# First loads in halves over two queues: x's first chunk and the first weights' columns, and the first products in halves, of a hybrid encoder

## The chip, the cores and the metric

The kernel runs on one core of a Trainium2 chip. A core has TensorE (PE, matrix products; the load of its stationary operand is shown as PEld), VectorE (DVE), ScalarE (ACT), GpSimd (POOL) and SyncE (SP), which mostly issues loads. ScalarE can issue loads too, through a queue of its own. The metric is the time of one execution on the device in microseconds (us); lower is better.

## The reference

The reference is a two-layer encoder trunk over 512 tokens of width 1024, in float32. The first layer mixes the tokens by a bidirectional gated linear attention, the second by grouped-query softmax attention with rotary positions. Each is followed by a gated MLP with a width-3 convolution. Before every sub-layer stands an RMS norm. Cut to the part that this change touches, the start of the first layer:

```python
h = rmsnorm(x, norm_mix[0])              # x: (1, 512, 1024)
proj = h @ gla_w_in                      # width 512 + 512 + 1024 + 1024 + 32
q, k, v, g, r = jnp.split(proj, ...)     # v and g: 1024 columns each
...
x = x + gla_mixer(h, ...)
x = x + conv_ffn(rmsnorm(x, norm_ffn[0]), ...)
```

## The kernel before, in words

x is held transposed, features in partitions, as eight chunks of 128 features by 512 tokens (`x[0]` to `x[7]`). Every product is made of three products in a fast 32-bit format (`F32R`): an operand is split into a rounded high part (`hi`, `wh`) and the remainder as low part (`lo`, `wl`), and high by high, high by low and low by high are summed. Of the norm, only the weight per feature is applied ahead of the products; the factor per token comes afterwards.

**The weights.** The class `Weights` loads blocks of 1 MB (`raw`, two buffers) and splits halves of them into `wh` and `wl` (three buffers each). The high part is a copy on ScalarE (line 143, one on VectorE at line 141 for the first), the low part a subtraction on VectorE (line 144).

**The start.** ScalarE's queue issues the load of the parameters `prm` (line 166), among them the norm's weights. SyncE's queue issues eight pairs of loads (lines 170 and 171): chunk c of x, and the 512 columns of the first weights that belong to chunk c. Each load has 256 KB. Each load counts up one of eight counters in turn, and an issue waits until the load before on its counter has landed. Meanwhile PE makes eight small warm-up products from constants (line 182), whose result also gives the constant `halfneg` (line 184, a copy on VectorE).

**The first products.** `gla` (line 343 on) makes the high part of chunk 0 (`norm.high`, line 231, ScalarE), splits the first weights (`W.make`), makes the low part (`norm.low`, line 236, VectorE) and goes on with the other seven chunks. The squares for the norm (line 240 on ScalarE, line 244 summed on VectorE) come beside it. `token_steps` makes the products `vg` (line 297) of the first 512 columns of v: for each chunk k of features, and each of four blocks j of 128 tokens, the block of x is PE's stationary operand and the weights' 512 columns are streamed; four banks collect the sums over all eight chunks. For the first two chunks the products stand by kind: four high by high, then four with `wl`, then four with the low part of x.

**What sets the order.** A scheduler places each engine's instructions by its own estimates of when their operands are ready; the program's order is a guide only. An instruction without inputs, such as the preload of a table of functions for ScalarE (in `gla` and in `attention`), can be placed far ahead. In the order built of the kernel before, the preload of `attention` coincides with the first one (line 411), and one load stands at the start.

Of the kernel before, what the change touches and what calls it, by code (L numbers as in the profile page):

```python
# [8 lines left out]
F32 = mybir.dt.float32  # L9
F32R = mybir.dt.float32r  # L10
U8 = mybir.dt.uint8
AF = mybir.ActivationFunctionType
ALU = mybir.AluOpType

P = 128
S = 512
D = 1024
KC = D // P
NT = S // P
# [27 lines left out]
def hybrid_encoder_kernel(  # L47
# [21 lines left out]
    pe, act, dve, pool, sync = nc.tensor, nc.scalar, nc.vector, nc.gpsimd, nc.sync  # L69
    mm = pe.matmul  # L70
# [7 lines left out]
    def nm(s):  # L78
        uid[0] += 1
        return f"{s}{uid[0]}"  # L80
# [6 lines left out]
    def pair(tag, bufs, dt, n):  # L87
        return sp.tile([P, 2 * S], dt, tag=tag, bufs=bufs, name=nm(n))
# [11 lines left out]
    x = [cp.tile([P, S], F32, name=f"x{c}") for c in range(KC)]  # L100
    prm = cp.tile([P, PC_N], F32, name="prm")

    class Weights:
# [10 lines left out]
        def make(self, key):  # L114
            src, i, h = key
            if h == 0 and (id(src), i) not in self.raw:
                t = sp.tile([P, 4 * S], F32, tag="raw", bufs=2, name=nm("raw"))
                sync.dma_start(t, src[i])
                self.raw[id(src), i] = t
            r = self.raw[id(src), i][:, h * 2 * S : (h + 1) * 2 * S]  # L120
            hi, lo = pair("wh", 3, F32R, "wh"), pair("wl", 3, F32R, "wl")
            if any(src is a and i < n for a, n in self.by_dma):
                act.activation(hi, r, AF.Copy)
                act.activation(lo, r, AF.Copy, scale=-1.0)
                self.pending.append((lo, r))
            else:
                self.split(hi, lo, r, 2 if src is w_vg and i < 2 else 1, src is w_vg and i == 0 and h == 0)
            self.made[id(src), i, h] = (hi, lo)

        def flush(self):  # L130
# [2 lines left out]
                pool.dma_start(lo.bitcast(F32), r, accum_op=ALU.add)  # L133
            self.pending = []

        def split(self, hi, lo, r, pieces, first):
            n = 2 * S // pieces
            for q in range(pieces):
                sl = slice(q * n, (q + 1) * n)
                if first and q == 0:  # L140
                    dve.tensor_copy(hi[:, sl], r[:, sl])
                else:
                    act.activation(hi[:, sl], r[:, sl], AF.Copy)  # L143
                dve.tensor_tensor(lo[:, sl], r[:, sl], hi[:, sl].bitcast(F32), ALU.subtract)  # L144

        def half(self, src, n):
            key = (id(src), n // 2, n % 2)
# [7 lines left out]
    W = Weights()  # L155
# [9 lines left out]

    act.dma_start(prm, par)
    raw = [sp.tile([P, 4 * S], F32, tag="raw", bufs=2, name=f"first{i}") for i in range(2)]
    for c in range(KC):
        r = slice((c % 4) * S, (c % 4 + 1) * S)
        sync.dma_start(x[c], xT[c * P : (c + 1) * P, :])  # L170
        sync.dma_start(raw[c // 4][:, r], w_vg[c // 4, :, r])
        W.raw[id(w_vg), c // 4] = raw[c // 4]

    ident = cp.tile([P, P], F32, name="ident")
    make_identity(nc, ident)
# [34 lines left out]
    class Norm:  # L210
# [15 lines left out]
        def weight(self, c):  # L226
            return prm[:, PC_NORM + self.idx * KC + c : PC_NORM + self.idx * KC + c + 1]

        def high(self, c):
            t = pair("xhl", 8, F32R, "xhl")  # L230
            act.activation(t[:, :S], x[c], AF.Copy, scale=self.weight(c))
            self.hl[c] = (t[:, :S], t[:, S:])

        def low(self, c):
# [48 lines left out]
    def token_steps(src, i0, hl, ps, width, per_half):  # L283

        for hf in range(KC // per_half):
            wh, wl = W.half(src, i0 + hf)

            late = src is w_vg and i0 > 0 and hf == 0
            for kk in range(per_half):
                todo = [(kk, j, i) for j in range(NT - late) for i in range(3)]  # L290
                if late and kk == 1:
                    todo += [(k, NT - 1, i) for k in range(2) for i in range(3)]
                if src is w_vg and i0 + hf * per_half + kk < 2:
                    todo.sort(key=lambda a: a[2])
                for a, j, i in todo:
                    k, sl = hf * per_half + a, slice(a * width, (a + 1) * width)
                    mm(ps[j][:, :width], hl[k][i == 2][:, j * P : (j + 1) * P], (wl if i == 1 else wh)[:, sl],  # L297
                       start=k == 0 and i == 0, stop=k == KC - 1 and i == 2)
                if kk == 1:
                    W.flush()  # L300
                yield

    def token_tiles(*a):
        for _ in token_steps(*a):
            pass
# [35 lines left out]


    def gla(norm, nxt):
        norm.high(0)
        W.make(W.todo.pop(0))
        norm.low(0)
        for c in range(1, KC):
# [7 lines left out]
        def seg(i, between=None):  # L355
            ps = [bank(tag, "vg") for tag in SEG_BANKS[i]]
            for n, _ in enumerate(token_steps(w_vg, i * 4, norm.hl, ps, S, 2)):
                if between is not None:
                    between(n)
            return ps  # L360
# [8 lines left out]
        ps = seg(0)  # L369
# [266 lines left out]
    def attention(norm, nxt):  # L636
# [74 lines left out]
        def kpair():  # L711
            head, ksc = yield from roped(0, PC_QK + 2, 1.0, "ksc")
            ky, kk = [head(0)], []
            yield
            ky.append(head(1))
            for e in range(2):
                yield
                ps = bcast_rows([ksc[:, 2 * j + e : 2 * j + e + 1].to_broadcast([P, P]) for j in range(NT)])
                dve.tensor_tensor(ky[e], ky[e], ps, ALU.mult)
                t = big(F32R, "k")  # L720
                split(ky[e], t)
                kk.append(t)
            return kk
# [3 lines left out]
        def qpair(i, tag="acc"):  # L727
            head, sc = yield from roped(1 + i, PC_QK, float(HD), "qsc", tag)
            for e in range(2):
                y = head(e)  # L730
                yield
                t = big(F32R, "q")
                split(y, t)
                heads[2 * i + e] = (t, sc, e)
                yield
# [17 lines left out]

        ps = [bank("acc" if j < 2 else "pt", "av") for j in range(NT)]
        vg2 = token_steps(w_av, 0, norm.hl, ps, 2 * HD, 4)
        run(qg, 2)
        run(vg2, 1)
# [50 lines left out]
        def mix(h, hf):  # L808
            ph3, pl3 = pts.pop((h, hf))
            vo = (h // 4) * HD  # L810
            if hf == 0:
                pos[h] = bank("po", "po")
            dst = pos[h][:, hf * 256 : (hf + 1) * 256]
            for k in range(NT):
                vsl = slice(k * 256 + vo, k * 256 + vo + HD)
                mm3(dst, vh[:, vsl], vl[:, vsl], ph3[:, k, :], pl3[:, k, :], k == 0, k == NT - 1)
            if hf == 1:
                t = big(F32R, "oT") if h < 4 else pair("xhl", 8, F32R, "oT")
                split(pos[h], t)
                oh[h] = (t[:, :S], t[:, S:])  # L820
# [26 lines left out]

    norms = [Norm(i) for i in range(4)]
    cw = gla(norms[0], norms[1])
    ffn(0, norms[1], cw, norms[2])  # L850
    attention(norms[2], norms[3])
# [82 lines left out]
```

## Time and profile before

| | |
|---|---|
| median of 3 runs | 1133.32 us (1133.29 to 1133.46) |
| the profiled execution | 1133.16 us |
| its span | 1131.4 us |
| PE busy | 1125.7 us |
| DVE busy | 690.1 us |
| ACT busy | 482.1 us |
| POOL busy | 76.0 us |

The span runs from the first instruction to the last of the profiled execution; the time of the execution has some more around it. In a row of the timeline stand start and busy time in us, the engine, the line of the kernel, the operation, its output and its inputs, the shapes, and in brackets the idle time of the engine before it with what ended it. Engines with a q behind their name (SPq, ACTq) are the issue of loads. Several equal instructions that follow each other share a row (x4).

### The profile page before, as it was taken

The page shows a single profiled execution, that of the slowest core. Times are in us where ns is not written, and L with a number is a line of the kernel's source. Part 1 is how long each engine was busy: PE and PEld are TensorE (multiplying, and loading weights), DVE is VectorE, ACT ScalarE, POOL GpSimd, SP SyncE. Part 2 cuts the span into 40 slices and gives each one's busy share as a digit, 9 for nine tenths or more (in the row PEclk, how much of TensorE's full clock was granted, in tenths as well). Part 3 has the DMA queues.
Part 4 walks back from the last instruction along what each step waited for, and adds up shares of the span by engine and source line. Part 5 has one row for each costly group of instructions (what it writes and reads, how often), then busy time and mean ns, then how long its engine had stood idle before and what let it go on. Part 6 is the DMA issues. An engine that isn't in the chain of part 4 may idle for free.

```text
span 1131.4 us, 12991 instructions
## 1 busy us (share of the span) xinstructions
PE 1125.7 (99%) x5260; PEld 939.2 (83%) x5260; DVE 690.1 (61%) x996; ACT 482.1 (43%) x690; POOL 76.0 (7%) x66
## 2 busy tenths in 40 slices
PE   9999999999999999999999999999999999999998
PEld 7888888888888888888888888888888888888887
DVE  6787563677777777633325589766777777762221
ACT  5564232444444444422234667644444444442210
POOL 0104110000000000000004433000000000000000
PEclk9999999999999999999999999999999999999999
DMA  6422211232322323223247633223232232323320
GB/s 231 149 75 78 84 63 38 75 112 75 112 97 90 112 75 112 100 86 112 77 152 181 149 76 75 56 75 112 75 112 85 101 112 75 112 84 121 130 93 19
DMA packets 19980, 111.66 MB, mean 99 GB/s; under 512 B 2384, under 2 KB 3024, under 8 KB 8400
## 3 DMA queue, kind: packets, MB, share of 16 engines
q1 hardware_dynamic: 17328, 102.29, 25.9%
q0 software_dynamic: 2304, 8.39, 3.9%
q8 instruction: 41, 0.67, 0.2%
q10 hardware_dynamic: 288, 0.15, 0.0%
q14 instruction: 19, 0.16, 0.0%
HBM read 100.34 MB, written 2.10 MB: 91 GB/s over the span
## 4 chain that ended last, share of the span: by engine, by line
PE 99%; DVE 0%; DMA 0%; ACT 0%; issue 0%; SPq 0%; DVEq 0%; ACTq 0%
PE up L266 14%; PE up L267 14%; PE up L268 14%; PE vg L297 8%; PE op L323 8%; PE dn L266 7%; PE dn L268 7%; PE dn L267 7%; PE o L548 2%; PE pt L802 1%; PE av L297 1%; PE kv L524 1%; PE A L266 1%; PE A L268 1%; PE A L267 1%; PE B L266 1%
## 5 line engine op out<-in xcount | busy, mean ns | idle before, releaser
L143 ACT ACTIVATE wh<-raw 128x1024 fp32r<-128x1024 f32 x164 | 173.3, 1056 | 351.4 <-PE up L267 132.8
L144 DVE TENSOR_TENSOR wl<-raw,wh 128x1024 fp32r<-128x1024 f32 x164 | 203.7, 1242 | 144.8 <-ACT wh L143 144.6
L266 PE MATMUL up<-xhl,wh 128*128 128x512 f32 x704 | 274.3, 390 | 0.0
L268 PE MATMUL up<-xhl,wl 128*128 128x512 f32 x704 | 273.9, 389 | 0.0
L267 PE MATMUL up<-xhl,wh 128*128 128x512 f32 x704 | 273.9, 389 | 0.0
L268 PEld LDWEIGHTS up<-xhl,wl 128*128 128x128 f32 x704 | 132.2, 188 | 27.6
L266 PEld LDWEIGHTS up<-xhl,wh 128*128 128x128 f32 x704 | 132.2, 188 | 27.4
L267 PEld LDWEIGHTS up<-xhl,wh 128*128 128x128 f32 x704 | 132.2, 188 | 27.1
L266 PE MATMUL dn<-gu,wh 128*128 128x512 f32 x352 | 136.9, 389 | 0.0
L267 PE MATMUL dn<-gu,wh 128*128 128x512 f32 x352 | 136.9, 389 | 0.0
L268 PE MATMUL dn<-gu,wl 128*128 128x512 f32 x352 | 136.9, 389 | 0.0
L603 DVE TENSOR_TENSOR u<-up,R 128x512 f32<-128x512 f32 x88 | 60.3, 687 | 52.7 <-PE up L268 52.7
L297 PE MATMUL vg<-wh,xhl 128*128 128x512 f32 x256 | 79.7, 390 | 0.6 <-DVE halfneg L184 0.6
L605 ACT ACTIVATE y<-u,cw 128x512 f32<-128x512 f32 x88 | 71.2, 811 | 20.4 <-DVE u L603 20.4
L268 PEld LDWEIGHTS dn<-gu,wl 128*128 128x128 f32 x352 | 66.1, 188 | 13.8
L267 PEld LDWEIGHTS dn<-gu,wh 128*128 128x128 f32 x352 | 66.1, 188 | 13.7
L266 PEld LDWEIGHTS dn<-gu,wh 128*128 128x128 f32 x352 | 66.1, 188 | 13.6
L323 PE MATMUL op<-oT,wh 128*128 128x512 f32 x256 | 70.9, 395 | 0.0
L607 DVE SCALAR_TENSOR_TENSOR y<-u,cw,y 128x511 f32<-128x511 f32 x88 | 65.9, 751 | 2.9
L606 DVE SCALAR_TENSOR_TENSOR y<-u,cw,y 128x511 f32<-128x511 f32 x88 | 65.6, 746 | 0.6 <-ACT y L605 0.6
L609 ACT ACTIVATE y<-y 128x512 f32<-128x512 f32 x44 | 27.9, 634 | 87.8 <-DVE y L607 87.8
L297 PEld LDWEIGHTS vg<-wh,xhl 128*128 128x128 f32 x256 | 48.0, 188 | 10.6 <-ACT sq L240 0.7
(186 smaller groups left out, 1432.1 us busy)
## 6 DMA issues: line engine op xcount, KB each, us to landing
raw<-in_w_up_dram SPq DMA_DIRECT2D x44, 1024.0 KB, 4.8
raw<-in_w_down_dram SPq DMA_DIRECT2D x22, 1024.0 KB, 4.8
wl<-raw POOLq DMA_DIRECT2D x16, 512.0 KB, 4.7
raw<-in_w_vg_dram SPq DMA_DIRECT2D x6, 1024.0 KB, 4.7
raw<-in_w_akq_dram SPq DMA_DIRECT2D x5, 1024.0 KB, 5.2
raw<-in_w_kq_dram SPq DMA_DIRECT2D x4, 1024.0 KB, 4.8
raw<-in_w_gout_dram SPq DMA_DIRECT2D x4, 1024.0 KB, 4.8
raw<-in_w_aout_dram SPq DMA_DIRECT2D x4, 1024.0 KB, 4.9
```

The costliest lines, as they stand in the source:

```text
L143: act.activation(hi[:, sl], r[:, sl], AF.Copy)
L144: dve.tensor_tensor(lo[:, sl], r[:, sl], hi[:, sl].bitcast(F32), ALU.subtract)
L266: mm(ps, wh, mh, start=start, stop=False)
L267: mm(ps, wh, ml, start=False, stop=False)
L268: mm(ps, wl, mh, start=False, stop=stop)
L297: mm(ps[j][:, :width], hl[k][i == 2][:, j * P : (j + 1) * P], (wl if i == 1 else wh)[:, sl], start=k == 0 and i == 0, stop=k == KC - 1 and ...
L323: mm(pss[ng][n], wt[:, sl], mv, start=k == 0 and i == 0, stop=k == KC - 1 and i == 2)
L603: dve.tensor_tensor(u, ps, norm.R, ALU.mult)
L605: act.activation(y, u, AF.Identity, scale=w(1), bias=w(3))
L606: dve.scalar_tensor_tensor(y[:, 1:], u[:, : S - 1], w(0), y[:, 1:], ALU.mult, ALU.add)
L607: dve.scalar_tensor_tensor(y[:, : S - 1], u[:, 1:], w(2), y[:, : S - 1], ALU.mult, ALU.add)
L609: act.activation(res[1], res[1], AF.Silu)
```

## The change

The loads of `x[0]` and of the first 512 columns of the weights are cut into halves of 256 columns, 128 KB each. SyncE's queue issues the first half of both, then all the other chunks as before; ScalarE's queue issues the second half of both, after the parameters. The rounding of the first weights on VectorE is done in two pieces; the subtraction for their low part stays one instruction over 512 columns and comes after both. The high part of chunk 0 of x is made in two pieces on ScalarE. The four first products high by high become eight products of 256 weight columns: for the first two token blocks the first columns and then the second ones, then the same for the other two token blocks.

In the order built, the warm-up products, the products after the first eight, and the instructions of GpSimd are the same as before. On ScalarE two issues of loads come before the table load; the first square stands behind the high part of chunk 1; and the preload of `attention` (the same table as the first) now stands by itself, ahead of the high part of chunk 7. On VectorE the copy of `halfneg` stands behind the first subtraction instead of ahead of it, and the first sum of squares behind the low part of chunk 2.

```diff
-                self.split(hi, lo, r, 2 if src is w_vg and i < 2 else 1, src is w_vg and i == 0 and h == 0)
+                cuts = [0, S, 2 * S] if src is w_vg and i < 2 else [0, 2 * S]
+                if src is w_vg and i == 0 and h == 0:
+                    for sl in (slice(0, S // 2), slice(S // 2, S)):
+                        dve.tensor_copy(hi[:, sl], r[:, sl])
+                    dve.tensor_tensor(lo[:, :S], r[:, :S], hi[:, :S].bitcast(F32), ALU.subtract)
+                    cuts = cuts[1:]
+                self.split(hi, lo, r, cuts)
...
-        def split(self, hi, lo, r, pieces, first):
-            n = 2 * S // pieces
-            for q in range(pieces):
-                sl = slice(q * n, (q + 1) * n)
-                if first and q == 0:
-                    dve.tensor_copy(hi[:, sl], r[:, sl])
-                else:
-                    act.activation(hi[:, sl], r[:, sl], AF.Copy)
-                dve.tensor_tensor(lo[:, sl], r[:, sl], hi[:, sl].bitcast(F32), ALU.subtract)
+        def split(self, hi, lo, r, cuts):
+            for a, b in zip(cuts, cuts[1:]):
+                act.activation(hi[:, a:b], r[:, a:b], AF.Copy)
+                dve.tensor_tensor(lo[:, a:b], r[:, a:b], hi[:, a:b].bitcast(F32), ALU.subtract)
...
-    for c in range(KC):
+    for queue, cols in ((sync, slice(0, S // 2)), (act, slice(S // 2, S))):
+        queue.dma_start(x[0][:, cols], xT[:P, cols])
+        queue.dma_start(raw[0][:, cols], w_vg[0, :, cols])
+    for c in range(1, KC):
+        sync.dma_start(x[c], xT[c * P : (c + 1) * P, :])
         r = slice((c % 4) * S, (c % 4 + 1) * S)
-        sync.dma_start(x[c], xT[c * P : (c + 1) * P, :])
         sync.dma_start(raw[c // 4][:, r], w_vg[c // 4, :, r])
...
-        def high(self, c):
+        def high(self, c, halves=False):
             t = pair("xhl", 8, F32R, "xhl")
-            act.activation(t[:, :S], x[c], AF.Copy, scale=self.weight(c))
+            for sl in ((slice(0, S // 2), slice(S // 2, S)) if halves else (slice(0, S),)):
+                act.activation(t[:, sl], x[c][:, sl], AF.Copy, scale=self.weight(c))
...
+                if src is w_vg and i0 + hf + kk == 0:
+                    for h, j in ((0, 0), (0, 1), (1, 0), (1, 1), (0, 2), (0, 3), (1, 2), (1, 3)):
+                        cols = slice(h * S // 2, (h + 1) * S // 2)
+                        mm(ps[j][:, cols], hl[0][0][:, j * P : (j + 1) * P], wh[:, cols], start=h == 0, stop=False)
+                    todo = todo[NT:]
...
-        norm.high(0)
+        norm.high(0, True)
```

More of the change, by code (lines that the diff above doesn't have):

```diff
@@ L167, in hybrid_encoder_kernel @@
     raw = [sp.tile([P, 4 * S], F32, tag="raw", bufs=2, name=f"first{i}") for i in range(2)]
-    for c in range(KC):
+    for queue, cols in ((sync, slice(0, S // 2)), (act, slice(S // 2, S))):
[3 more added lines that the diff above has]
+        sync.dma_start(x[c], xT[c * P : (c + 1) * P, :])
         r = slice((c % 4) * S, (c % 4 + 1) * S)
-        sync.dma_start(x[c], xT[c * P : (c + 1) * P, :])
         sync.dma_start(raw[c // 4][:, r], w_vg[c // 4, :, r])
-        W.raw[id(w_vg), c // 4] = raw[c // 4]
+    for i in range(2):
+        W.raw[id(w_vg), i] = raw[i]
     ident = cp.tile([P, P], F32, name="ident")
```

## The prediction

> **What bounds the kernel now.** I read the page's span, then its chain of work that ended last, then the chain in order of time for where its first link lies, then the timeline of the first 30 us.
>
> ```profile
> span 1131.4 us, 12991 instructions
> ...
> PEclk9999999999999999999999999999999999999999
> ...
> PE 99%; DVE 0%; DMA 0%; ACT 0%; issue 0%; SPq 0%; DVEq 0%; ACTq 0%
> ```
>
> The chain is TensorE (PE) for 99% of the span. So an edit counts only if it moves the moment at which PE's stream begins, adds PE work, or opens a gap in the stream. The first pieces of the chain in order of time (start, length):
>
> ```profile
> 1.24 3.63 DMA first<-in_w_vg_dram
> 5.46 22.04 PE vg L297 x96
> ```
>
> The first link is the load of the first weights' columns; then 96 products run without a pause from 5.46 to 27.50. All that the change touches lies before that stream or in its first few us, so what PE gains or loses at its first group of products is what the whole kernel gains or loses. The timeline there (start, busy time, engine):
>
> ```profile
> 0.81 0.41 ACTq L166 DMA_DIRECT2D prm<-in_par_dram  x1
> ...
> 1.24 0.42 SPq L171 DMA_DIRECT2D first<-in_w_vg_dram  x1
> 1.24 1.28 ACT L411 ACT_TABLE_LOAD   x1 [1.24 <-PEq L924]
> ...
> 1.27 3.62 PE L182 MATMUL warm<-two 128*128 128x128 f32 x16 [1.27 <-DVE bd L188]
> ...
> 1.71 0.42 SPq L170 DMA_DIRECT2D x<-in_xT_dram  x1
> ...
> 3.87 0.72 ACT L231 ACTIVATE xhl<-x,prm 128x512 fp32r<-128x512 f32 x1 [1.34 <-DMA prm<-in_par_dram]
> ...
> 4.89 0.43 DVE L141 CAST wh<-first 128x512 fp32r<-128x512 f32 x1 [3.43 <-DMA first<-in_w_vg_dram]
> ...
> 5.23 0.16 DVE L184 COPY halfneg<-warm 128x8 f32<-128x8 f32 x1
> ...
> 5.35 0.69 DVE L144 TENSOR_TENSOR wl<-first,wh 128x512 fp32r<-128x512 f32 x1
> 5.43 0.76 PEld L297 LDWEIGHTS vg<-wh,xhl 128*128 128x128 f32 x4 [0.74 <-ACT sq L240]
> 5.46 1.17 PE L297 MATMUL vg<-wh,xhl 128*128 128x512 f32 x4 [0.58 <-DVE halfneg L184]
> 5.96 0.75 DVE L236 SCALAR_TENSOR_TENSOR xhl<-x,prm,xhl 128x512 fp32r<-128x512 f32 x1
> ...
> 6.47 1.08 PE L297 MATMUL vg<-wl,xhl 128*128 128x512 f32 x4
> ...
> 7.39 1.99 PE L297 MATMUL vg<-wh,xhl 128*128 128x512 f32 x8
> ```
>
> The rounding of the weights (CAST) ends at 5.32 and PE starts 0.14 later; the activations' part was ready at 4.59. The warm-up products hold PE until 4.89, so PE idles for only 0.57 us. The last group of products that the change cuts is followed by the `wl` group at 6.47; that moment is my mark. From there a full product starts every 0.227 us (4 from 6.47 to 7.39).
>
> When each load landed, from the DMA view over one issue at a time (its last column is us from issue to landing):
>
> ```profile
> x<-in_xT_dram SPq DMA_DIRECT2D x1, 256.0 KB, 2.8
> prm<-in_par_dram ACTq DMA_DIRECT2D x1, 22.0 KB, 3.0
> ...
> first<-in_w_vg_dram SPq DMA_DIRECT2D x1, 256.0 KB, 3.6
> ...
> x<-in_xT_dram SPq DMA_DIRECT2D x1, 256.0 KB, 4.5
> ...
> first<-in_w_vg_dram SPq DMA_DIRECT2D x1, 256.0 KB, 5.0
> ```
>
> With the issues at 0.81, 0.81, 1.24, 1.71 and 2.17 they landed at 3.6 (x chunk 0), 3.8 (parameters), 4.84 (weight columns 0), 6.2 (x chunk 1) and 7.2 (columns 1). The loads wait for bandwidth, not for their issue: 256 KB more takes 1.0 to 1.4 us.
>
> **The change, part by part.**
>
> *Earlier first product.* The first 256 columns of x and of the weights (128 KB each) need 256 KB to have come instead of 512. That is the byte count at which x chunk 0 landed, 3.6; ScalarE's queue now takes its share beside them, so I put the second of the two (w0a) at 3.9, between 3.6 and 4.84 and nearer to the row with as many bytes. A cast of 256 columns is estimated at 0.29 us, midway between 0.43 for 512 and 0.16 for 8, and done at 4.25. The activations' half still waits for the parameters (3.8), which stay first in ScalarE's queue; half of 0.72 and an overhead give some 0.45, so 4.3. Both are ready before the warm-up ends at 4.89. So PE's first product moves from 5.46 to about 4.9, and no further: that caps the gain near 0.57 us, 0.05% of the time.
>
> *Eight half products for four.* The trace has 256-column products of this kind later, in the values' projection of the attention:
>
> ```profile
> 613.38 0.48 PE L267 MATMUL B<-xhl,wh 128*128 128x512 f32 x1
> 613.70 0.39 PE L268 MATMUL B<-xhl,wl 128*128 128x512 f32 x1
> 613.93 0.28 PE L297 MATMUL av<-wh,xhl 128*128 128x256 f32 x1
> 614.05 0.28 PE L297 MATMUL av<-wl,xhl 128*128 128x256 f32 x1
> 614.17 0.41 PE L297 MATMUL av<-wh,xhl 128*128 128x256 f32 x2
> 614.41 0.28 PE L297 MATMUL av<-wl,xhl 128*128 128x256 f32 x1
> ```
>
> Four in 0.48, so 0.12 each with another stationary tile every time; eight take 0.96 against 0.91 for four full ones: 0.05 more. The first product after another kind costs 0.1 extra (613.38 to 613.70 is 0.32), as it does before (5.46 to 6.47 is 1.01). Without a wait inside, the `wl` mark would come at 4.9 + 0.96 + 0.1 = 5.96, a gain of 0.51.
>
> *The second halves on ScalarE's queue.* The third product needs columns 256 to 511 of the weights (w0b). They are the third DMA of ScalarE's queue, issued near 1.73 (0.81 plus two steps of 0.46, about that from 1.24 to 1.71 on SyncE's queue), beside SyncE's x chunk 1 at 1.71. Its landing L is the one unknown that decides. From L: the cast starts 0.05 later, takes 0.29, PE follows after 0.11 and has six half products left (0.72): L + 1.17. The other way is as long: 0.05 + 0.29 + 0.03, then the subtraction over all 512 columns, which now waits for the second cast, 0.69, and 0.11: L + 1.17. So the mark is at L + 1.17, against 6.47: break-even is L = 5.30. Lower bound: 4.84, the landing of the whole columns before, if nothing of chunk 1 gets in between: mark 6.01, gain 0.46. Upper bound: 6.2, that of x chunk 1, if both queues are served in turn so that w0b ends together with the x chunk 1 issued at the same moment: mark 7.37, loss 0.90. The parameters speak for the upper one: 22 KB alone in the other queue, issued with x chunk 0, landed 0.2 us after its 256 KB, so a transfer in ScalarE's queue did not pass one that was issued beside it. I take L = 5.8, two thirds of the way up: mark 6.97, loss 0.5.
>
> The Trainium skill's page "DMA: Bandwidth & Descriptors" (Rules for kernel authors) speaks against this edit: issuing from several engines gives no bandwidth, since all run on the same DMA engines and interleave. By it the sum would be a loss of 0.9; by the order of issue alone it would be a gain of 0.46; the parameters' row agrees with the page.
>
> *What is queued behind.* On VectorE behind the late subtraction (ends at L + 1.06 = 6.86): the 0.16 copy, then the low part of x chunk 0, 0.75, done at 7.8; PE wants it at 6.97 + 0.91 = 7.88. No second gap, but next in line. On ScalarE two more DMA issues push the table load to some 2.2 to 3.5, still before the parameters (3.8). In the order built, the first square now stands after chunk 1's high part instead of before it:
>
> ```profile
> 6.21 0.72 ACT L231 ACTIVATE xhl<-x,prm 128x512 fp32r<-128x512 f32 x1 [1.11 <-DMA x<-in_xT_dram]
> ...
> 7.37 0.61 ACT L143 ACTIVATE wh<-first 128x512 fp32r<-128x512 f32 x1
> ...
> 8.24 0.68 DVE L144 TENSOR_TENSOR wl<-first,wh 128x512 fp32r<-128x512 f32 x1
> ```
>
> One square (0.62) follows 6.21 either way, so chunk 1's weights are rounded at 7.98 as before; PE wants them at 6.97 + 1.82 = 8.8. Two more DMAs also move SyncE's third weight load behind the parameters' landing (its counter is one of eight in turn): issue 3.85 instead of some 3.1 (four steps of 0.47 after 1.24). Columns 1, issued at 2.17, land at 7.2, so that queue still holds work then: nothing.
>
> *A second table load.* In the order built, the attention's table preload, merged with the first before, stands on ScalarE ahead of chunk 7's high part: 1.28 us, by the row above.
>
> ```profile
> 15.98 0.71 ACT L231 ACTIVATE xhl<-x,prm 128x512 fp32r<-128x512 f32 x1
> ...
> 17.39 1.29 DVE L144 TENSOR_TENSOR wl<-first,wh 128x512 fp32r<-128x512 f32 x2
> ...
> 18.60 2.21 DVE L244 TENSOR_TENSOR sq<-sq,sq 128x512 f32<-128x512 f32 x3
> ...
> 24.62 0.39 PE L297 MATMUL vg<-wh,xhl 128*128 128x512 f32 x1
> ...
> 27.35 0.95 PE L252 MATMUL ms<-ones,sq 128*128 128x1 f32 x8
> ```
>
> Chunk 7's parts are ready at 16.7 and 18.7, and PE takes them from 24.62; the squares' sum is ready at 20.8, and PE takes it at 27.35. Some 6 us of cover hide 1.3; uncovered it would cost 1.28.
>
> **Sum.** The profiled execution took 1133.16: the span of 1131.4 and 1.76 around it, 0.16 under the median of the runs, 1133.32. On it: +0.5, so 1133.66; beside the median, 1133.8. A difference under 0.2% (2.27 us) is about what a measurement of this kernel cannot tell from no change.
>
> **Rivals.**
> 1. *The second halves come as early as whole columns did.* For it: the bytes ahead in order of issue are the same 512 KB. Against: x chunk 1 is issued at the same moment. Gain 0.46 to 0.51: 1132.8 to 1132.9. Chance 0.28.
> 2. *The first product does not move at all:* the warm-up holds PE, or the first half lands after 4.6. With L at 5.8 the time is the forecast's, since the third product waits anyway; with L early it is 1133.3. Chance 0.08.
> 3. *Slower by more than 0.2%: the clock stays low.* One product pass of 128 columns in f32 took 3.62/16 = 0.226 in the warm-up and half of that later:
>
> ```profile
> 174.32 1.79 PE in L501 x16
> ```
>
> So PE ran the warm-up at half speed and was at full speed by 6.47, though the page's granted clock (PEclk) is at its top throughout. The new pause (after two half products at about 5.2, until L + 0.45 = 6.25) falls right where the speed rises. If it kept PE at half speed for another stretch as long as the warm-up (3.6 us), the stream would lose 1.8 beside the 0.5: 1135.6, just at the bound; it decides from there on. Against: a pause of 0.57 at the same place did no harm. Chance 0.04, half of it beyond the bound. The Trainium skill's "TensorE: Matmul & The Clock Gate" (Part 1) gives such a mechanism, a clock halved until a window of some 3.4 us was busy and dropped only after an idle one; by it a pause of 1 us after the rise costs nothing, and one before the rise could.
>
> **How the numbers follow.** Forecast (second halves late, loss 0 to 0.9): 0.60, with 1133.3 to 1134.2 as its own range. With rival 1 below and something for a still later L (columns 1's landing, 7.2, would give a loss of 1.9, 1135.2, little chance), the range is 1132.8 to 1134.5. No case gains over 0.57, so faster by 0.2% has 0.01; slower, from rival 3 and an uncovered second table load together with a late L, 0.03; the same 0.96.
>
> **What would show it.** PE's first `vg` product near 4.9; a wait of about 1 us after two half products, ended by the second cast on VectorE, itself waiting for ScalarE's queue's load; the first `wl` product near 6.97; half products 0.12 apart; no idle PE after that up to 27; a table load near 14 to 16 with nobody waiting. The forecast is wrong if w0b lands before 5.3 (then `wl` stands before 6.47), or if half products run 0.24 apart, at half speed.

## The result

The changed kernel takes 1135.4 us (median of 22 runs, 1133.78 to 1135.92), the kernel before 1133.32 (22 runs, 1133.0 to 1133.88): a ratio of 1.0014, 95% interval 1.0008 to 1.002, so slower by 0.14%. (The ratio goes by all the runs; the two medians alone would give 1.0018.) The median hides what happened. The 22 times fall into two groups with nothing between them: ten from 1133.78 to 1134.11 and twelve from 1135.32 to 1135.92. The forecast, 1133.8, is the lower group; its range ended at 1134.5, and the upper group lies beyond it.

The profile of the changed kernel is of a run of the lower group (1133.87; span 0.7 longer than before). Its page and the first pieces of its chain in order of time:

```profile
span 1132.1 us, 13005 instructions
...
PE 99%; DVE 0%; DMA 0%; ACT 0%; ACTq 0%; issue 0%; DVEq 0%
```

```profile
1.73 4.47 DMA first<-in_w_vg_dram
6.57 0.98 PE vg L308 x6
7.54 20.89 PE vg L312 x92
```

The chain now begins with ScalarE's load, issued at 1.73 and landed at 6.20. When each load landed is issue plus the last column, from the DMA view over the first issues (weights' first half, x's second half, x chunk 1, weights' second half; issued at 1.24, 1.25, 1.71 and 1.73):

```profile
first<-in_w_vg_dram SPq DMA_DIRECT2D x1, 128.0 KB, 3.4
x<-in_xT_dram ACTq DMA_DIRECT2D x1, 128.0 KB, 3.7
...
x<-in_xT_dram SPq DMA_DIRECT2D x1, 256.0 KB, 4.3
...
first<-in_w_vg_dram ACTq DMA_DIRECT2D x1, 128.0 KB, 4.5
```

So the first half of the weights came at 4.6, only 0.2 before the whole columns did in the kernel before (4.84), and the second half at 6.2, 0.2 after the x chunk 1 that was issued beside it. The timeline:

```profile
1.26 3.78 PE L189 MATMUL warm<-two 128*128 128x128 f32 x16 [1.26 <-DVE bd L195]
...
4.67 0.29 DVE L130 CAST wh<-first 128x256 fp32r<-128x256 f32 x1 [3.22 <-DMA first<-in_w_vg_dram]
...
5.12 0.47 PE L308 MATMUL vg<-wh,xhl 128*128 128x256 f32 x2
...
6.22 0.29 DVE L130 CAST wh<-first 128x256 fp32r<-128x256 f32 x1 [1.25 <-DMA first<-in_w_vg_dram]
6.55 0.69 DVE L131 TENSOR_TENSOR wl<-first,wh 128x512 fp32r<-128x512 f32 x1
6.57 0.98 PE L308 MATMUL vg<-wh,xhl 128*128 128x256 f32 x6 [0.98 <-DVE wh L130]
...
7.38 1.10 PE L312 MATMUL vg<-wl,xhl 128*128 128x512 f32 x4
...
8.33 1.98 PE L312 MATMUL vg<-wh,xhl 128*128 128x512 f32 x8
...
10.14 1.07 PE L312 MATMUL vg<-wl,xhl 128*128 128x512 f32 x4
```

Two half products run at 5.12, 0.34 earlier than the first product before; then PE idles for 0.98 us until the second rounding, and the `wl` group starts at 7.38 instead of 6.47: 0.91 later. From there PE runs without a pause, a product every 0.227 us (8 from 8.33 to 10.14), so the loss stays: the sums of squares' products start at 28.28, 0.93 later than in the kernel before (27.35). At the end of the span 0.7 of it is left; where the rest comes back stays open. The upper group needs another cause, of some 1.8 us more; the experiments look for it.

### The profile page after: what moved, and what is told of

It reads as the page before. It is cut to its first block, busy times and chain, and to the rows that moved or that the text cites. A ratio compares the mean times of both kernels' runs of the same rounds, so it can differ in the third digit from the quotient of the medians.

```text
span 1132.1 us, 13005 instructions
## 1 busy us (share of the span) xinstructions
PE 1126.0 (99%) x5264; PEld 939.6 (83%) x5264; DVE 690.1 (61%) x997; ACT 483.5 (43%) x692; POOL 75.9 (7%) x66
## 4 chain that ended last, share of the span: by engine, by line
PE 99%; DVE 0%; DMA 0%; ACT 0%; ACTq 0%; issue 0%; DVEq 0%
PE up L276 14%; PE up L275 14%; PE up L274 14%; PE op L338 8%; PE vg L312 8%; PE dn L275 7%; PE dn L274 7%; PE dn L276 7%; PE o L563 2%; PE pt L817 1%; PE av L312 1%; PE kv L539 1%; PE A L274 1%; PE A L276 1%; PE A L275 1%; PE B L274 1%
```

## The experiments

Two theories for the upper group stood against each other: that the pause sometimes keeps PE's clock at half speed for one more stretch (A), or that the second half of the weights sometimes lands still later (B).

### The changed kernel once more, and two single runs of it

No edit: the same kernel in 11 runs, then in two single runs, each with its profile.

> The changed kernel once more. Its 22 runs fall into two groups, ten near 1133.9 us and twelve near 1135.7, and the profile shown of it is one of the first group. Theory A (PE's clock): the pause of 1.2 us after the first two half products, at 5.4 to 6.6, sometimes keeps PE at half speed for one more stretch of about 3.5 us; the runs again fall into two groups 1.7 to 1.9 apart, and a profile of the upper group shows the 512-column products after 6.6 some 0.43 us apart for about 3.5 us, with the second weights' half landing at about 6.2 as in the lower group. Theory B (the load): in the upper group the second half of the weights lands 1.8 us later, near 8.0, and the products after it are 0.227 apart as always.

> The changed kernel, one look, to have the profile of a run of the upper group (1135.3 or more; about one run in two). Theory A (clock): the second half of the weights lands at 6.1 to 6.4 and the products after it are 0.43 us apart up to some 10 us. Theory B (late load): it lands near 8 and products are 0.227 apart.

> As the look before it: the changed kernel, for the profile of a run of the upper group, with the same two expectations.

The 11 runs: six from 1133.82 to 1134.17, five from 1135.38 to 1135.73; ratio to before 1.0012 (1.0003 to 1.0021). Their profile is of the lower group once more. The two single runs took 1135.89 and 1135.65, so both profiles are of the upper group. Over all 35 runs, 19 are in the upper group. Timeline of the first single run:

```profile
5.45 0.77 PE L308 MATMUL vg<-wh,xhl 128*128 128x256 f32 x2 [0.40 <-DVE wh L130]
...
6.28 0.29 DVE L130 CAST wh<-first 128x256 fp32r<-128x256 f32 x1 [0.98 <-DMA first<-in_w_vg_dram]
...
6.63 1.65 PE L308 MATMUL vg<-wh,xhl 128*128 128x256 f32 x6 [0.41 <-DVE wh L130]
...
8.08 1.91 PE L312 MATMUL vg<-wl,xhl 128*128 128x512 f32 x4
...
9.79 2.52 PE L312 MATMUL vg<-wh,xhl 128*128 128x512 f32 x8
...
12.15 1.09 PE L312 MATMUL vg<-wl,xhl 128*128 128x512 f32 x4
```

The second half of the weights is rounded at 6.28, as in the lower group (6.22). But the six half products take 1.45 us instead of 0.81 (6.63 to 8.08, against 6.57 to 7.38), and the four `wl` products start 0.43 apart (8.08 to 9.79 is 1.71). Only in the next group of eight (2.36 instead of 1.81) do they go over to 0.227. PE runs at half speed until about 10.7, 4.1 us after the pause, and loses half of that: the sums of squares' products, right after the first 96, start at 28.28 in the lower group's profile and at 30.30 here, 2.02 later. Theory B falls; the half speed of theory A is seen directly. The second single run shows the same, with full speed from about 10.2:

```profile
7.99 1.91 PE L312 MATMUL vg<-wl,xhl 128*128 128x512 f32 x4
...
9.69 2.27 PE L312 MATMUL vg<-wh,xhl 128*128 128x512 f32 x8
```

The pauses of the first single run are not longer than the lower group's. PE stands idle for 0.40 and 0.41 us, in two pieces, where the lower group's profile has one piece of 0.98, because the first half of the weights came later (rounded at 5.01, against 4.67) and the two early half products take 0.77 instead of 0.47. So the length of one pause does not tell the groups apart.

Through all of it the view by stretches shows the granted clock of the first single run at its top:

```profile
6.60:8.00 1.40, 1.37 (x6) 1.37 (x7) 1.39 (x4) 1.40 (x4) 0.00 (x0) 1.00 1.05 405
8.00:9.70 1.70, 1.70 (x6) 1.40 (x5) 1.70 (x4) 1.70 (x4) 0.00 (x0) 1.00 1.03 368
```

(PE's busy time and number of instructions come first behind the length; the granted clock is the 1.00 near the end.) The number of products tells it: six touch the second stretch of 1.70 us, two of them still half products, and in the lower group ten do. Neither the busy time nor that clock does.

### The pause filled with warm-up products

```diff
+    for i in range(4):
+        mm(warm[:, P : 2 * P], two[:, :P], two[:, P : 2 * P], start=i == 0, stop=i == 3)
     for i in range(8):
         mm(warm[:, :P], two[:, :P], two[:, P : 2 * P], start=i == 0, stop=i == 7)
```

> The changed kernel with four more warm-up products ahead of the eight, so that PE stays busy until 5.7 to 6.6 and the pause before the third half product shrinks from 1.2 us to under 0.9. Theory A (clock): the upper group vanishes or becomes rare; the median falls to 1133.8 to 1134.0, 0.6 over before. Theory B (late load): two groups as before, median where the changed kernel's is.

> The changed kernel with four more warm-up products, one look more: theory A (clock) again expects a time of 1133.7 to 1134.4 and no 512-column products 0.43 apart; a time near 1135.7 would mean that a pause under 0.5 us can do the same harm.

1134.04 (11 runs, 1133.68 to 1134.44), ratio 1.0006 (0.9997 to 1.0015); the single run took 1134.02. None of the 12 runs is in the upper group, with the same loads in the same queues. Its timeline:

```profile
3.13 3.07 PE L191 MATMUL warm<-two 128*128 128x128 f32 x16
...
5.96 1.29 PE L310 MATMUL vg<-wh,xhl 128*128 128x256 f32 x8
...
7.09 1.11 PE L314 MATMUL vg<-wl,xhl 128*128 128x512 f32 x4
```

The warm-up lasts until the half products start at 5.96, and the first one no longer starts at 5.1: that early start had gained nothing. What is left is the late second half, 0.7 us. So it is PE's idle time that makes the upper group: in the single run the first half of the weights came as late as in the upper group (rounded at 4.94), and PE was at full speed from about 5.2 even so.

### The kernel before with two warm-up products

```diff
-    dve.memset(two[:, :P], 2.0 ** -5)
-    dve.memset(two[:, P : 2 * P], -(2.0 ** -6))
+    dve.memset(two[:, :P], 2.0 ** -4)
+    dve.memset(two[:, P : 2 * P], -(2.0 ** -5))
...
-    for i in range(8):
-        mm(warm[:, :P], two[:, :P], two[:, P : 2 * P], start=i == 0, stop=i == 7)
+    for i in range(2):
+        mm(warm[:, :P], two[:, :P], two[:, P : 2 * P], start=i == 0, stop=i == 1)
```

> The kernel before with two warm-up products instead of eight (their constants scaled so that the result is the same): no load and no product of the change, but PE idle from about 2.1 until 5.46. Theory A (clock): the first products run at half speed for up to 3.5 us, 0.43 apart, and the time is 1.2 to 1.8 us over before, 1134.5 to 1135.1. Theory B (late load): the load is that of before, so the time stays within 0.2 us of before, 1133.3.

1135.22 (11 runs, 1134.1 to 1136.14), ratio 1.0016 (1.0007 to 1.0025): 1.9 us lost at the median without any edit to loads or products. The runs spread over 2 us without a clear gap.

```profile
1.26 1.22 PE L182 MATMUL warm<-two 128*128 128x128 f32 x4 [1.26 <-DVE bd L188]
...
4.97 2.04 PE L297 MATMUL vg<-wh,xhl 128*128 128x512 f32 x4 [2.49 <-DVE wh L141]
...
6.81 1.91 PE L297 MATMUL vg<-wl,xhl 128*128 128x512 f32 x4
```

In this run the weights even came earlier, and the first four products started at 4.97; but they take 1.84 us up to 6.81, 0.46 each. In this case PE's speed at the start depends on how busy it was before, and eight warm-up products were what kept the kernel before out of this.

### The change's loads, with whole products

```diff
-                if src is w_vg and i0 + hf + kk == 0:
-                    for h, j in ((0, 0), (0, 1), (1, 0), (1, 1), (0, 2), (0, 3), (1, 2), (1, 3)):
-                        cols = slice(h * S // 2, (h + 1) * S // 2)
-                        mm(ps[j][:, cols], hl[0][0][:, j * P : (j + 1) * P], wh[:, cols], start=h == 0, stop=False)
-                    todo = todo[NT:]
```

> The changed kernel with its loads and pieces of rounding as they are, but the first four products whole (512 columns) as in the kernel before. PE then has nothing between the warm-up's end at 5.0 and the second half of the weights at 6.2: a pause of 1.6 us. Theory A (clock): as many or more runs in the upper group than of the changed kernel, median 1135.4 to 1136, lower group at 1133.8 to 1134.0; in an upper run the first products are 0.43 apart. If the half products themselves were what slows the kernel, this one is at 1133.3 to 1133.6 in one group.

1135.8 (11 runs, 1135.59 to 1136.08), ratio 1.0022 (1.0012 to 1.0031): all 11 runs as slow as the upper group, none near the lower.

```profile
7.05 2.05 PE L305 MATMUL vg<-wh,xhl 128*128 128x512 f32 x4 [2.00 <-DVE wh L130]
...
8.89 1.57 PE L305 MATMUL vg<-wl,xhl 128*128 128x512 f32 x4
```

Behind a pause of 2.00 us the first products of this profile are slow (0.46 apart from 7.05). Not all of the loss is the clock's: here the second half of the weights also came later than in the lower group (rounded at 6.61, against 6.22), and whole products must wait for it. At full speed the same start would have brought the `wl` group at 8.06, 1.59 behind the kernel before, so some 1135.0 as an estimate (1133.39 and 1.59); the fastest of the 11 runs took 1135.59. So the other ten, which have no profile, were most likely slow too. The half products are not what slows the changed kernel: without the two early ones none of 11 runs was fast, with them 16 of 35 were.

### All halves on SyncE's queue

```diff
-    for queue, cols in ((sync, slice(0, S // 2)), (act, slice(S // 2, S))):
+    for queue, cols in ((sync, slice(0, S // 2)), (sync, slice(S // 2, S))):
```

> The changed kernel with the second halves on SyncE's queue, right behind the first halves, so that chunk 1 of x comes after them. If the two queues being served in turn is what made the second half of the weights land at 6.2: it lands near 4.9, the pause after the first half products is under 0.4 us, the wl products start near 6.0 to 6.2 and the time is one group at 1132.8 to 1133.1, 0.2 to 0.5 under before. If it is the halving itself (512 rows of 1 KB instead of 256 of 2 KB) or the number of loads: it lands at 6 or later and the time is 1133.9 or more.

1133.65 (11 runs, 1133.35 to 1134.14), ratio 1.0002 (0.9993 to 1.0011): one group, but not the gain that was expected.

```profile
3.75 0.29 DVE L130 CAST wh<-first 128x256 fp32r<-128x256 f32 x1 [2.30 <-DMA first<-in_w_vg_dram]
...
5.17 0.29 DVE L130 CAST wh<-first 128x256 fp32r<-128x256 f32 x1
...
6.04 0.69 DVE L131 TENSOR_TENSOR wl<-first,wh 128x512 fp32r<-128x512 f32 x1
...
6.78 1.20 PE L312 MATMUL vg<-wl,xhl 128*128 128x512 f32 x4 [0.35 <-DVE wl L131]
```

The halves come in time: the weights are rounded at 3.75 and 5.17, against 4.67 and 6.22 with two queues. The pause is gone, and with it the upper group. What eats the gain is the scheduler's order: it put the low part of x chunk 0 ahead of the subtraction on VectorE, so that this starts at 6.04 instead of some 5.5, and `wl` starts at 6.78, 0.31 behind the kernel before. A second loss follows, since x chunk 1 now comes behind the second halves: its high part is made at 6.96 instead of 6.21, and PE waits for the rounding of chunk 1's weights on ScalarE.

```profile
8.78 0.76 PEld L312 LDWEIGHTS vg<-wh,xhl 128*128 128x128 f32 x4 [0.32 <-ACT wh L144]
```

By the sums of squares, at 28.00, this profile is 0.65 behind the kernel before.

### All halves on SyncE's queue, the weights' second half ahead of x's

```diff
-    for queue, cols in ((sync, slice(0, S // 2)), (act, slice(S // 2, S))):
-        queue.dma_start(x[0][:, cols], xT[:P, cols])
-        queue.dma_start(raw[0][:, cols], w_vg[0, :, cols])
+    sync.dma_start(x[0][:, : S // 2], xT[:P, : S // 2])
+    sync.dma_start(raw[0][:, : S // 2], w_vg[0, :, : S // 2])
+    sync.dma_start(raw[0][:, S // 2 : S], w_vg[0, :, S // 2 : S])
+    sync.dma_start(x[0][:, S // 2 :], xT[:P, S // 2 :])
```

> The changed kernel with all four halves on SyncE's queue in the order x first half, weights first half, weights second half, x second half. In the order built the subtraction for wl stands again right behind the two casts (with both halves on SyncE's queue in the other order it stood behind the low part of x), and one product with wl stands among the eight half products. The second half of the weights should land near 4.7 and wl be ready near 5.9, so the four wl products end at 7.2 to 7.4 (7.38 in the kernel before): 1133.1 to 1133.4, one group, no gain to speak of. A time over 1133.6 would speak for the halving itself as a cost.

1133.13 (11 runs, 1132.74 to 1133.47) beside 1133.39 of the kernel before, measured together with it (20 runs), ratio 0.9998 (0.9989 to 1.0007): the interval holds no change, and the kernel before reached the same median, 1133.13, at another time.

```profile
4.26 0.29 DVE L130 CAST wh<-first 128x256 fp32r<-128x256 f32 x1 [0.24 <-DMA first<-in_w_vg_dram]
...
4.59 0.69 DVE L131 TENSOR_TENSOR wl<-first,wh 128x512 fp32r<-128x512 f32 x1
4.65 0.72 PE L309 MATMUL vg<-wh,xhl 128*128 128x256 f32 x4
...
7.13 2.10 PE L313 MATMUL vg<-wh,xhl 128*128 128x512 f32 x8
...
9.83 0.63 ACT L144 ACTIVATE wh<-first 128x512 fp32r<-128x512 f32 x1 [0.81 <-DMA first<-in_w_vg_dram]
...
11.25 0.50 PE L313 MATMUL vg<-wl,xhl 128*128 128x512 f32 x1
```

Both halves are rounded by 4.55, and PE's next group of full products starts at 7.13 instead of 7.39. That lead of 0.26 us does not last: ScalarE then waits 0.81 us for the weights of a later chunk, and the `wl` product at 11.25 starts at the same moment as in the kernel before. The sums of squares start at 27.48, against 27.35. So halving the first loads and products brought no lasting gain in this profile, even in the best order of the loads that was tried; that the medians also differ by 0.26 lies within the noise.

### The kernel before with nine warm-up products

```diff
+    mm(warm[:, P : 2 * P], two[:, :P], two[:, P : 2 * P], start=True, stop=True)
     for i in range(8):
```

> The kernel before with one more warm-up product, so that PE is busy until 5.1 to 5.3 and its pause before the first product at 5.46 falls from 0.57 us to some 0.2; loads and products as before. In the order built the first subtraction stands one place earlier on VectorE, ahead of the copy of halfneg. If the clock's rise also varies in the kernel before, whose runs spread over 1132.6 to 1133.9 with one at 1135.6, no run should come near 1135 and the median fall by 0 to 0.3. If it costs anything (the copy of halfneg, the products) the time is 0.2 or more over before.

1133.31 (11 runs, 1132.77 to 1133.76) beside 1133.13 (15 runs, 1132.67 to 1133.77), ratio 1.0001 (0.9992 to 1.001): nothing that can be measured. Its profile (a run of 1133.57) shows something else:

```profile
5.13 1.88 PE L298 MATMUL vg<-wh,xhl 128*128 128x512 f32 x4
6.85 1.09 PE L298 MATMUL vg<-wl,xhl 128*128 128x512 f32 x4
```

PE had worked without a pause from 1.26 on, and still the first four products take 1.72 us, 0.43 apart; full speed comes only at about 6.7. In the kernel before the warm-up's last products were already shorter, at about 4.5. Between these two lie the other profiles without a long pause: about 5.2 and 5.4 with twelve warm-up products, 5.5 with all halves on SyncE's queue. So the moment of the rise moves by some 2 us from profile to profile, even without a pause, and though PE's work is the same in all of them up to about 4.6. Here it cost 0.4 us (the sums of squares start at 27.75, against 27.35), although the weights had come 0.39 earlier.

One of 33 runs of the kernel before, measured at another time, was at 1135.58. Whether that was a late rise of the clock too stays open; it has no profile.

## Why the prediction was wrong, point by point

*Earlier first product.* The move was right, its size was not: 5.12 and 4.94 in two profiles of the lower group, 5.45 and 5.34 in two of the upper, against the 4.9 forecast. The first half of the weights was put at 3.9 and landed at 4.6. With loads in ScalarE's queue beside it, it was rounded at 4.50 to 5.34 in seven profiles; the whole columns were at 4.40 to 4.89 in the three profiles with the loads of the kernel before. So over two queues the first half came no earlier than the whole had. With all halves on SyncE's queue it was rounded at 3.75.

*Eight half products.* As forecast at full speed: six took 0.81 us, which is 0.12 each and once the 0.1 extra behind a pause. The sum from L left that 0.1 out; PE followed the cast after 0.06 instead of 0.11, and the cast the landing after 0.02 instead of 0.05. The slips cancel, so that 1.17 came out (1.18) by some luck.

*The second halves on ScalarE's queue.* The mechanism was right, and the term was undersized: the landing was put at 5.8 and came at the upper bound, 6.2, 0.2 after x chunk 1 (6.0). The mark came at 7.38 against 6.97, a loss of 0.91 against 0.5; L + 1.17 gives 7.37. With the second halves on SyncE's queue the same weights were rounded 1.05 (5.17) or 1.96 us (4.26) sooner. So it is not the size of the pieces. This term of the sum was mis-sized by 0.4. That the lower group's times, 0.6 over the kernel before, lie so near the forecast's 0.5 is luck: the mark was 0.91 late and the sums of squares 0.93, and a part of that does not show in the time. The rule of the Trainium skill's "DMA: Bandwidth & Descriptors" (Rules for kernel authors), that transfers from several issuing engines only interleave, gave the better sum here, 0.9; the 0.91 agrees.

*What is queued behind, and the second table load.* As forecast: no second pause up to the sums of squares, and nobody waited for the table load:

```profile
15.58 1.28 ACT L652 ACT_TABLE_LOAD   x1
...
16.87 0.72 ACT L239 ACTIVATE xhl<-x,prm 128x512 fp32r<-128x512 f32 x1
...
18.55 0.69 DVE L145 TENSOR_TENSOR wl<-first,wh 128x512 fp32r<-128x512 f32 x1
...
28.28 0.94 PE L260 MATMUL ms<-ones,sq 128*128 128x1 f32 x8
```

*The step that failed: rival 3, the clock that stays low.* Its place (the new pause) and its price (1.8 us beside the loss, 1135.6) were those of the upper group, 1135.7. What failed is its chance, 0.04, where 19 of 35 runs showed it; with so small a chance it was left out of the range. The argument against it was that a pause of 0.57 us did no harm at the same place. But that pause did not stand at the same place: in that profile the clock had risen before it. The last warm-up product of the kernel before, and then of the changed kernel's first profile:

```profile
4.61 0.27 PE L182 MATMUL warm<-two 128*128 128x128 f32 x1
```

```profile
4.63 0.42 PE L189 MATMUL warm<-two 128*128 128x128 f32 x1
```

The middle ones take 0.42 in both, so the shorter 0.27 means full speed by 4.6; the 0.57 us without work began at 4.89. It says nothing of idle time ahead of the rise. In the changed kernel the clock had not risen by 4.63, and PE had only two half products to do until about 6.6. In the lower group's two profiles it rose by then (by 5.12 in one; in the other the two half products still take 0.77, and the next six, from 6.68 on, run at full speed). In the upper group's two it had not, and full speed came at 10.2 and 10.7; the six half products ran 0.24 apart there (1.45 us in all), which the prediction had named as a sign of being wrong. With the pause filled, none of 12 runs was hit; with 2.00 us of it, most likely all 11. A mechanism that the profile showed so plainly, with an edit that puts idle time where the speed rises, deserved far more than 0.04.

What sorts a single run into one group or the other stays open. The moment of the rise moves from profile to profile; but in the four profiles the first half of the weights also came later in the upper group (rounded at 4.90 and 5.01, against 4.50 and 4.67), and no run separates the two. The Trainium skill's "TensorE: Matmul & The Clock Gate" (Part 1) says that the window in which PE must be busy runs freely, so that the moment of the rise differs from run to run of one kernel. The rises between 4.5 and 6.7 us without a long pause agree with that; the window itself is in no trace here.

## What to carry to other kernels

Before a first load is cut in two, ask which transfers will run beside the second piece: here, in a queue of its own, it landed 0.2 us after a transfer of twice its size that was issued beside it, and the first piece came no earlier than the whole had. At the start of a kernel, keep PE busy until its real products can run without a pause; here a product that started early and was followed by a wait gained nothing, and the wait of some 1 us could cost 2.0 more. To see where full speed begins, read the lengths and distances of equal products, of the warm-up too: an unharmed pause counts as evidence only on the same side of the rise. And give a mechanism that comes or goes by chance a range with two groups, since a median near an even split can land in either.

## What was not expected of the hardware

Idle time of about 1 us in PE's first 7 us cost up to 2.0 us more than itself, and only in some runs of the same program. The half speed lasted until about 10.7 in the first single run's profile. Without any pause it lasted until about 4.5 in one profile and 6.7 in another. The profile's granted clock stayed at 1.00 all the while; the distance between the starts of equal products (0.43 against 0.227) showed it. Two loads issued 0.02 us apart on two queues, of 256 and 128 KB, landed 0.2 us apart, at 6.0 and 6.2.
